# Second attention's scores: two full-height passes over stacked halves in place of three half-height passes

## The chip, the cores and the metric

The kernel runs on one core of one Trainium2 chip. The metric is the device time of one execution in microseconds (us), as the median of several runs. TensorE is called PE in the profile and its weight loads PEld; VectorE is DVE, ScalarE is ACT, GpSimd is POOL, SyncE is SP.

## What is computed

The reference runs a first block of two layers on 512 tokens of width 1024 (with 256 context tokens) and then a second block. The change lies in the attention of the second block, which has 8 dilated heads and 8 forgetting heads ("fox"), all of width 64:

```python
proj = h @ w_in[layer]
qa, ka, va, qf, kf, vf, f_pre = jnp.split(proj, splits, axis=-1)
o_dil = _dilated_attention(heads(qa, 8), heads(ka, 8), heads(va, 8), rel_bias)
log_f = jax.nn.log_sigmoid((f_pre + b_forget[layer]).astype(jnp.float32))
o_fox = _forgetting_attention(heads(qf, 8), heads(kf, 8), heads(vf, 8), log_f)
# inside, per query block of 128:
s = jnp.einsum('bqhd,bkhd->bhqk', qi, k) * SCALE      # the scores
s = s + ci[..., None] - c_k[:, :, None, :]            # fox; the dilated heads add a bias by distance
p = jax.nn.softmax(jnp.where(k_pos[None, :] <= q_pos[:, None], s, NEG_INF), axis=-1)
o = jnp.einsum('bhqk,bkhd->bqhd', p, v)
```

Behind it come an output projection, a router and 32 experts (two of which each token uses), and a final normalisation.

## The kernel before, in words

Matrix products that need more than one fp32r pass are split: a value x is held as hi (x rounded to fp32r) and lo (x - hi), and the product is hi·hi + lo·hi + hi·lo, three matmuls into one accumulator (`mm3`, L218 to L222: the lines L220, L221 and L222 are the three passes, whatever the product).

The second attention is `second_attention` (L1224). Its heads are taken two at a time, as groups g = 0 to 7 (0 to 3 dilated, 4 to 7 forgetting), a head being a step (g, e). All is written out straight, without loops on the chip. A compile-time scheduler lays out the order on each engine from the program's order and its own estimates of time; each engine then runs its queue in order, and waits on semaphores for its data. Only later, in the expert stage, is PE's order written out by hand.

- `late_consts` (L1186) makes `tri` (L1191, a triangle of ones for a cumulative sum) and `mask` from an index tile `jp`, which has the buffer tag `sqo`.
- `values` (L1196) projects the values of all heads. The forget gates' cumulative sum is `pcum` (L1260), which reads `tri`; its negative goes to `cs` (L1262) and by DMA to `cd`.
- `proj(g, a)` (L1270) projects the queries (a = 0) or the keys (a = 1) of one group: 24 matmuls of 128 x 512 into PSUM (`pqk`), then one ACT instruction to hi (L1281) and one DVE instruction to lo (L1282), each over 128 partitions: head e's 64 rows are partitions 64e to 64e + 63.
- `Fill` (L61) spreads the matmuls of the projections of later groups and, at the end, of half of the output projection (`dil_out`) between the steps of the heads, so that PE has other work while a head's softmax runs. `need(g)` forces what a head's scores require.
- `head_scores` (L1377) does one head: it loads F (the bias row, or the cumulative sums) by DMA on SP into one of two buffers, then the scores for four query blocks i with 128 (i + 1) keys each, three passes of 64 rows; forgetting heads add `mask` on the diagonal block by one more matmul with the identity, 128 rows high (L1399). DVE adds F and takes the maximum (L1406), ACT takes the exponential (L1408), POOL divides by the sum (L1411).
- `head_out` (L1414) turns the probabilities (`pPT`, L1425), splits them into PT2h (ACT) and PT2l (DVE), and multiplies by the values (`pO`, L1434). The scores of the next head are issued ahead of the transposes of this one.
- `nil` (L1330), also with the tag `sqo`, is filled with zeros by POOL and written by 16 DMAs on SP to `yd`, which the experts add to later. The loads of weights (`wraw`, L211) go through the same SP queue.

Of the kernel before, what the change touches and what calls it, by code (L numbers as in the profile page):

```python
# [10 lines left out]
F32 = mybir.dt.float32  # L11
F32R = mybir.dt.float32r
I32 = mybir.dt.int32
U32 = mybir.dt.uint32
AF = mybir.ActivationFunctionType
OP = mybir.AluOpType
# [95 lines left out]
class K:  # L112
# [1073 lines left out]
    def late_consts(self):  # L1186

        nc, pool = self.nc, self.bp
        jp = pool.tile([128, 512], F32, name="jp", tag="sqo", bufs=1)
        nc.gpsimd.iota(jp, pattern=[[1, 512]], base=0, channel_multiplier=-1, allow_small_or_imprecise_dtypes=True)  # L1190
        self.tri = pool.tile([128, 512], F32R, name="tri")  # L1191
        nc.vector.tensor_scalar(self.tri, jp, 0.0, None, op0=OP.is_ge)
        self.mask = pool.tile([128, 128], F32R, name="mask")
        nc.vector.tensor_scalar(self.mask, jp[:, :128], 0.0, -1e30, op0=OP.is_gt, op1=OP.mult)
# [29 lines left out]
    def second_attention(self, hT):  # L1224
        nc, I, sp = self.nc, self.I, self.sp
# [10 lines left out]
        for s, nm, n in ((0, "b_router_group_2", 4), (4, "b_router_expert_2", 32)):  # L1236
            a = I[nm][0]
# [11 lines left out]
        e = bp.tile([128, 4, 8], F32, name="fe")  # L1249
# [7 lines left out]
        p = self.pt("pcum")  # L1257
        for t in range(4):
            for k, x in enumerate((zh, zl)):
                nc.tensor.matmul(p[:8, t * 128:512], x[:, t, :], self.tri[:, :512 - t * 128],  # L1260
                                 start=(t == 0 and k == 0), stop=(t == 3 and k == 1))
        cs = bp.tile([8, 512], F32, name="cs")  # L1262
        nc.vector.tensor_scalar(cs, p[:8], -1.0, None, op0=OP.mult)
        cd = self.dr.tile([8, 512], F32, name="cd")
        nc.sync.dma_start(cd, cs)


        qk = [[None, None] for _ in range(8)]

        def proj(g, a):  # L1270
            c = (1536 if g >= 4 else 0) + a * 512 + (g % 4) * 128
            w = self.wunit(wi[:, :, c:c + 128], [128, 8, 128])
            yield 0
            p = self.pc("pqk")
            for k in range(8):
                self.mm3(p, [x[:, k, :] for x in w], [h[:, k, :] for h in hT], k == 0, k == 7)
                yield 0.64
            hi = bp.tile([128, 512], F32R, name="qk2h", tag=f"qh{a}", bufs=2)
            lo = bp.tile([128, 512], F32R, name="qk2l", tag=f"ql{a}", bufs=2)
            s = 1.0 if a else 0.125  # L1280
            nc.scalar.activation(hi, p, AF.Copy, scale=s)  # L1281
            nc.vector.scalar_tensor_tensor(lo, p, s, hi.bitcast(F32), op0=OP.mult, op1=OP.subtract)  # L1282
            qk[g][a] = (hi, lo)


        wo = I["w_out_2"][0].rearrange("(k p) n -> p k n", p=128)
# [2 lines left out]
        def dil_out(c0, t):  # L1289
# [5 lines left out]
            for k in range(4):  # L1295
# [3 lines left out]
            nc.vector.scalar_tensor_tensor(x, p, rsh[0][:, t:t + 1], x, op0=OP.mult, op1=OP.add)  # L1299

        late = Fill([proj(g, a) for g in range(8) for a in range(2)]
                    + [dil_out(c0, t) for c0 in (0, 512) for t in range(4)])

# [73 lines left out]
    def head_scores(self, g, e, qk, cd):  # L1377

        nc, sp, bp = self.nc, self.sp, self.bp
        fox = g >= 4  # L1380
        Q, Kt = qk
        b = e * 64
        hh = (g % 4) * 2 + e
        F = bp.tile([128, 512], F32, name="F", tag="F", bufs=2)
        if fox:
            s = cd[hh:hh + 1, :]
            nc.sync.dma_start(F, bass.AP(tensor=s.tensor, offset=s.offset, ap=[[0, 128], [1, 512]]))
        else:
            s = self.fd[hh]
            nc.sync.dma_start(F, bass.AP(tensor=s.tensor, offset=s.offset + 127, ap=[[639, 128], [1, 512]]))  # L1390
        P = bp.tile([128, 1280], F32, name="P2", tag="P2", bufs=2)
        p2, p3, p1 = (self.pb("pS2") for _ in range(3))
        pS = [p1[:, 0:128], p1[:, 128:384], p2[:, 0:384], p3]
        at = (0, 128, 384, 768)
        for i in (2, 3, 1, 0):
            L = 128 * (i + 1)
            self.mm3(pS[i], [x[b:b + 64, i * 128:(i + 1) * 128] for x in Q], [x[b:b + 64, :L] for x in Kt], True, not fox)
            if fox:
                nc.tensor.matmul(pS[i][:, i * 128:L], self.identr, self.mask, start=False, stop=True)  # L1399
        m = sp.tile([128, 4], F32, name="m2", bufs=3)  # L1400
        l = sp.tile([128, 4], F32, name="l2", bufs=3)
        Ps = [P[:, at[i]:at[i] + 128 * (i + 1)] for i in range(4)]
        for i in (2, 3, 1, 0):
            L = 128 * (i + 1)
            o = 0 if fox else 384 - 128 * i
            nc.vector.tensor_tensor_reduce(Ps[i], pS[i], F[:, o:o + L], 1.0, -3e38, OP.add, OP.max, m[:, i:i + 1])  # L1406
            nc.vector.tensor_scalar(m[:, i:i + 1], m[:, i:i + 1], -1.0, None, op0=OP.mult)  # L1407
            nc.scalar.activation(Ps[i], Ps[i], AF.Exp, bias=m[:, i:i + 1], accum_out=l[:, i:i + 1])  # L1408
        for i in (2, 3, 1, 0):
            nc.vector.reciprocal(l[:, i:i + 1], l[:, i:i + 1])  # L1410
            nc.gpsimd.tensor_scalar(Ps[i], Ps[i], l[:, i:i + 1], 1.0, op0=OP.mult, op1=OP.mult)  # L1411
        return Ps
# [751 lines left out]
```

## Time and profile before

| | us |
|---|---|
| median of 3 runs | 1468.28 |
| lowest, highest | 1463.38, 1468.56 |
| the profiled execution, its own time | 1465.97 |
| its span in the trace | 1464.0 |
| PE busy | 1335.9 (91%) |
| DVE busy | 951.9 (65%) |
| ACT busy | 595.9 (41%) |
| POOL busy | 310.0 (21%) |

The second attention from its first scores' projections to the last head takes the trace from about 884 to 1087 us, the dilated heads up to 979. "Busy" counts an instruction from its start to its modelled end; PE's matmuls overlap one another, so that two starts in a row tell more of a matmul's cost than its printed duration. A trailing bracket in a row gives the idle time of the engine before it and what ended it; "issue" means that nothing which the profile shows was waited for. [...]

### The profile page before, as it was taken

How to read it: one execution, taken by the hardware profiler on the slowest of the kernel's cores; microseconds unless marked ns; L12 is line 12 of the kernel's file. 1: busy time of each engine (PE TensorE's matmuls, PEld its weight loads, DVE VectorE, ACT ScalarE, POOL GpSimd, SP SyncE). 2: the span in 40 equal slices, each digit the busy share in tenths (PEclk: the TensorE clock that was granted, in tenths of full speed). 3: DMA queues.
4: the chain of work that ended last, by engine and by line, in shares of the span. 5: the costliest groups of instructions: out<-in, count | busy, mean ns of one | idle time of the engine just before them, and what ended most of it. 6: DMA issues, size and time to landing. Idle time of an engine off the chain costs nothing. (4 is left out here: it accounts for less than half of the span.)

```text
span 1464.0 us, 22692 instructions
## 1 busy us (share of the span) xinstructions
PE 1335.9 (91%) x8094; PEld 1055.6 (72%) x8094; DVE 951.9 (65%) x2253; ACT 595.9 (41%) x1166; POOL 310.0 (21%) x396
## 2 busy tenths in 40 slices
PE   4999989998979999799999899999998899999873
PEld 2888778876858788678877697887877777575441
DVE  4789986665743779998784545655567543454555
ACT  4543254534641564266572435654444111112112
POOL 2332042322220323133231201211110111111101
PEclk9999999999999999999999999999998899999987
DMA  8643453444142435433334454223436689999971
GB/s 297 191 134 101 116 153 116 128 121 150 45 143 63 123 95 160 126 94 105 89 109 144 135 177 127 73 80 115 165 113 233 199 295 365 378 368 391 383 278 58
DMA packets 166918, 246.48 MB, mean 168 GB/s; under 512 B 46774, under 2 KB 102918, under 8 KB 166804
## 3 DMA queue, kind: packets, MB, share of 16 engines
q1 hardware_dynamic: 161460, 235.07, 48.5%
q0 software_dynamic: 4768, 7.84, 1.9%
q10 hardware_dynamic: 576, 2.10, 0.4%
q8 instruction: 65, 1.06, 0.3%
q14 instruction: 49, 0.40, 0.1%
HBM read 221.74 MB, written 33.33 MB: 174 GB/s over the span
## 5 line engine op out<-in xcount | busy, mean ns | idle before, releaser
L184 DVE TENSOR_TENSOR wlo<-wraw,whi 128x1024 fp32r<-128x1024 f32 (+3 forms) x98 | 118.9, 1219 | 67.5 <-ACT whi L183 66.9
L183 ACT ACTIVATE whi<-wraw 128x1024 fp32r<-128x1024 f32 (+3 forms) x98 | 100.6, 1035 | 116.6 <-PE pout L222 42.6
L922 POOL TENSOR_SCALAR P<-P,ll 128x768 f32<-128x768 f32 (+1 forms) x80 | 76.2, 957 | 186.5 <-DVE ll L921 104.2
L220 PE MATMUL pcm<-hTh,whi 128*128 128x256 f32 (+1 forms) x288 | 102.9, 357 | 10.4 <-DVE oa L529 4.3
L569 DVE SCALAR_TENSOR_TENSOR za<-zp,vec,za 128x783 f32<-128x783 f32 (+1 forms) x120 | 109.2, 917 | 0.5
L222 PE MATMUL pcm<-hTh,wlo 128*128 128x256 f32 (+1 forms) x288 | 99.6, 346 | 0.2 <-DVE wlo L184 0.2
L221 PE MATMUL pcm<-hTl,whi 128*128 128x256 f32 (+1 forms) x288 | 98.7, 343 | 0.0
L184 DVE TENSOR_TENSOR PTl<-pPT,PTh 128x512 fp32r<-128x512 f32 x104 | 70.4, 683 | 23.7 <-ACT PTh L183 23.3
L183 ACT ACTIVATE PTh<-pPT 128x512 fp32r<-128x512 f32 x104 | 60.3, 595 | 54.9 <-PE pPT L935 46.9
L920 ACT ACTIVATE P<-pS,nm 128x768 f32<-128x768 f32 (+1 forms) x80 | 64.9, 814 | 34.5 <-DVE nm L918 30.1
L1411 POOL TENSOR_SCALAR P<-P,l 128x384 f32<-128x384 f32 (+1 forms) x64 | 33.3, 532 | 205.0 <-DVE m L1407 153.1
L1805 POOL DMA_INDIRECT xg<-h2d,tok x32 | 31.6, 988 | 208.3 <-PE pturn L1789 131.7
L917 DVE TENSOR_REDUCE nm<-pS 128x1 f32<-128x768 f32 (+1 forms) x80 | 66.4, 844 | 14.2 <-PE pS L222 13.4
L220 PEld LDWEIGHTS pcm<-hTh,whi 128*128 128x128 f32 x288 | 55.3, 192 | 18.2 <-DVE oa L529 4.9
L220 PE MATMUL pcm<-hT0h,whi 128*128 128x512 f32 x144 | 59.5, 413 | 7.9 <-DVE oa L529 5.8
L935 PE MATMUL pPT<-ident,P 128*128 128x128 f32 x416 | 63.4, 280 | 3.6 <-POOL P L922 2.9
L1822 PE MATMUL pgu<-exT,eraw 128*128 128x128 f32 x512 | 61.1, 280 | 0.0
L1822 PEld LDWEIGHTS pgu<-exT,eraw 128*128 128x128 f32 x512 | 59.5, 195 | 1.3 <-DVE exT L1800 0.6
L222 PEld LDWEIGHTS pcm<-hTh,wlo 128*128 128x128 f32 x288 | 55.2, 192 | 6.5 <-DVE wlo L184 0.6
L221 PEld LDWEIGHTS pcm<-hTl,whi 128*128 128x128 f32 x288 | 55.2, 192 | 4.8 <-issue 0.2
L221 PE MATMUL pcm<-hT0l,whi 128*128 128x512 f32 x144 | 58.1, 404 | 0.0
L222 PE MATMUL pcm<-hT0h,wlo 128*128 128x512 f32 x144 | 58.1, 403 | 0.0
(533 smaller groups left out, 3691.3 us busy)
## 6 DMA issues: line engine op xcount, KB each, us to landing
wraw<-in_w_in_dram SPq DMA_DIRECT2D x56, 512.0 KB
eraw<-in_w_expert_gate_dram SPq DMA_DIRECT2D x52, 512.0 KB
eraw<-in_w_expert_up_dram SPq DMA_DIRECT2D x52, 512.0 KB
wraw<-in_w_mod_dram SPq DMA_DIRECT2D x48, 512.0 KB
wl<-in_w_expert_down_dram SPq DMA_DIRECT2D x32, 512.0 KB
wh<-in_w_expert_down_dram SPq DMA_DIRECT2D x32, 512.0 KB
wraw<-in_w_out_dram SPq DMA_DIRECT2D x24, 512.0 KB
wraw<-in_w_expert_gate_dram SPq DMA_DIRECT2D x12, 512.0 KB
```

Of the source, the lines that this page charges most:

```text
L183: nc.scalar.activation(hi, src, AF.Copy)
L184: return (eng or nc.vector).tensor_tensor(lo, src, hi.bitcast(F32), op=OP.subtract)
L220: mm(out, lhs[0], rhs[0], start=start, stop=False)
L221: mm(out, lhs[0], rhs[1], start=False, stop=False)
L222: mm(out, lhs[1], rhs[0], start=False, stop=stop)
L569: nc.vector.scalar_tensor_tensor(a[:, :nz], z[:, k:k + nz], cfw[:, i, k:k + 1], a[:, :nz], op0=OP.mult, op1=OP.add)
L917: nc.vector.tensor_reduce(nm, S, axis=AX.X, op=OP.max, negate=True)
L920: nc.scalar.activation(P, S, AF.Exp, bias=nm, scale=SM1, accum_out=l)
L922: nc.gpsimd.tensor_scalar(P, P, l, 0.5, op0=OP.mult, op1=OP.mult)
L935: nc.tensor.transpose(p[:, jj, i * 128:(i + 1) * 128], Ps[i][:, (j + jj) * 128:(j + jj + 1) * 128], self.ident)
L1411: nc.gpsimd.tensor_scalar(Ps[i], Ps[i], l[:, i:i + 1], 1.0, op0=OP.mult, op1=OP.mult)
L1822: self.last = self.nc.tensor.matmul(p[:, s, c, :], gu[2 * s + k // 4][:, k % 4, c * 128:(c + 1) * 128], x[:, k, :], start=(k == 0), stop=( ...
```

## The change

A head's query tile becomes 128 rows high: its hi over its lo. The keys' hi is written twice, into the upper and the lower half of a tile; the keys' lo lies over zeros in one of three fixed tiles whose lower halves are zeroed once. Then queries times (hi, hi) gives hi·hi + lo·hi in one pass, and queries times (lo, 0) gives hi·lo in a second. The evacuation of a projection is done in halves of 64 partitions, one for each head, two of them moving rows from partitions 64 to 127 down to 0 to 63 or up. There are four query tiles and three key-hi tiles in rotation. `tri` and `cs` move into the two buffers of F, and a tile `zero` comes between `jp` and `nil` in the buffer `sqo`.

```diff
-        self.tri = pool.tile([128, 512], F32R, name="tri")
+        self.tri = pool.tile([128, 512], F32R, name="tri", tag="F", bufs=2)
...
-        cs = bp.tile([8, 512], F32, name="cs")
+        cs = bp.tile([128, 512], F32, name="cs", tag="F", bufs=2)[:8]
...
         qk = [[None, None] for _ in range(8)]
+        klo = [bp.tile([128, 512], F32R, name=f"klo{i}") for i in range(3)]
+        zero = bp.tile([128, 512], F32, name="zero", tag="sqo", bufs=1)
+        nc.gpsimd.memset(zero, 0.0)
+        for t in klo:
+            nc.vector.tensor_copy(t[64:128], zero[64:128])
...
-            hi = bp.tile([128, 512], F32R, name="qk2h", tag=f"qh{a}", bufs=2)
-            lo = bp.tile([128, 512], F32R, name="qk2l", tag=f"ql{a}", bufs=2)
+
+            x = [bp.tile([128, 512], F32R, name="qk2", tag=f"qk{a}", bufs=4 - a) for e in range(2)]
+            y = [klo[(2 * g + e) % 3] for e in range(2)] if a else [t[64:128] for t in x]
             s = 1.0 if a else 0.125
-            nc.scalar.activation(hi, p, AF.Copy, scale=s)
-            nc.vector.scalar_tensor_tensor(lo, p, s, hi.bitcast(F32), op0=OP.mult, op1=OP.subtract)
-            qk[g][a] = (hi, lo)
+            for e in range(2):
+                r = p[64 * e:64 * e + 64]
+                nc.scalar.activation(x[e][0:64], r, AF.Copy, scale=s)
+                if a:
+                    nc.scalar.activation(x[e][64:128], r, AF.Copy)
+                nc.vector.scalar_tensor_tensor(y[e][0:64], r, s, x[e][0:64].bitcast(F32), op0=OP.mult, op1=OP.subtract)
+            qk[g][a] = list(zip(x, y))
...
-        Q, Kt = qk
-        b = e * 64
+        Q, Kt = qk[0][e][0], qk[1][e]
...
-            self.mm3(pS[i], [x[b:b + 64, i * 128:(i + 1) * 128] for x in Q], [x[b:b + 64, :L] for x in Kt], True, not fox)
+            for k in range(2):
+                nc.tensor.matmul(pS[i], Q[:, i * 128:(i + 1) * 128], Kt[k][:, :L], start=(k == 0), stop=(k == 1 and not fox))
```

## Rows read from the trace of the kernel before

**Rows 1.** Windows by stage: us, each engine's busy time, PEclk, DMA share, GB/s

```profile
884.00:979.00 95.00, 93.78 (x487) 75.84 (x487) 56.18 (x183) 51.10 (x118) 16.56 (x32) 1.00 0.30 81
979.00:1087.00 108.00, 108.00 (x521) 85.73 (x519) 63.48 (x199) 52.49 (x119) 17.27 (x33) 0.94 0.33 113
...
1250.00:1350.00 100.00, 97.06 (x768) 63.94 (x760) 45.26 (x85) 17.25 (x33) 15.17 (x16) 1.00 1.02 381
```

**Rows 2.** Waits of PE and its loads, 884 to 1087: total us, times, longest

```profile
PEld pS L1399 <- issue: 4.9, 16, 0.4
PEld pS L220 <- issue: 4.7, 13, 0.4
...
PEld pPT L1425 <- POOL P L1411: 1.2, 1, 1.2
PEld pO L1434 <- ACT PT2h L183: 1.1, 2, 0.6
...
PEld pS L220 <- ACT qk2h L1281: 0.7, 2, 0.4
```

**Rows 3.** Timeline of PE, one dilated head's scores: start us, duration us, instruction

```profile
943.24 0.39 PE L221 MATMUL pqk<-hT1l,whi 128*128 128x512 f32 x1
943.47 0.40 PE L222 MATMUL pqk<-hT1h,wlo 128*128 128x512 f32 x1
943.80 0.44 PE L220 MATMUL pS<-qk2h 64*128 64x384 f32 x1
944.08 0.33 PE L221 MATMUL pS<-qk2l,qk2h 64*128 64x384 f32 x1
...
944.43 0.39 PE L220 MATMUL pS<-qk2h 64*128 64x512 f32 x1
...
945.13 0.27 PE L220 MATMUL pS<-qk2h 64*128 64x256 f32 x1
...
945.48 0.22 PE L220 MATMUL pS<-qk2h 64*128 64x128 f32 x1
945.53 0.28 PE L221 MATMUL pS<-qk2l,qk2h 64*128 64x128 f32 x1
945.65 0.27 PE L222 MATMUL pS<-qk2h,qk2l 64*128 64x128 f32 x1
945.85 0.33 PE L1425 MATMUL pPT<-ident,P 128*128 128x128 f32 x1
```

**Rows 4.** Timeline of PE and PEld, one forgetting head's scores

```profile
979.43 0.44 PE L220 MATMUL pS<-qk2h 64*128 64x384 f32 x1
...
983.01 0.40 PE L1425 MATMUL pPT<-ident,P 128*128 128x128 f32 x2
...
979.43 0.18 PEld L220 LDWEIGHTS pS<-qk2h 64*128 64x128 f32 x1 [0.36 <-issue]
...
980.15 0.19 PEld L1399 LDWEIGHTS pS<-mask,identr 128*128 128x128 f32 x1 [0.25 <-issue]
```

**Rows 5.** Windows of 1 us, PE alone: us, busy, PEclk, DMA share, GB/s

```profile
984.00:985.00 1.00, 1.00 (x5) 0.50 0.02 6
```

**Rows 6.** Groups by line and form, 884 to 1090: busy us, mean ns, idle before

```profile
L1281 ACT ACTIVATE qk2h<-pqk 128x512 fp32r<-128x512 f32 x15 | 8.9, 592 | 0.2
L1448 ACT ACTIVATE oT<-pO 64x512 f32<-64x512 f32 x15 | 8.9, 594 | 18.7 <-PE pO L1434 18.6
...
L1449 DVE TENSOR_TENSOR oT<-pO,oT 64x512 f32<-64x512 f32 x15 | 10.2, 679 | 8.3 <-ACT oT L1448 8.0
```

**Rows 7.** Timeline of SP, ACT and DVE around the stage's start

```profile
855.15 29.18 SPq L211 DMA_DIRECT2D wraw<-in_w_in_dram  x9
885.92 0.30 SPq L1265 DMA_DIRECT2D cd<-cs  x1
...
874.05 2.96 ACT L183 ACTIVATE whi<-wraw 128x1024 fp32r<-128x1024 f32 x3 [0.34 <-PE pv L222]
...
892.75 0.56 DVE L1406 CUSTOM_DVE_ANT_0 P<-pS,F 128x384 f32<-128x384 f32 x1 [1.30 <-PE pS L222]
```

## Prediction

> **What bounds the kernel now.** I read the windows by stage first. In the eight dilated heads (884 to 979 us) PE is busy 93.78 of 95 us, in the eight forgetting heads (979 to 1087) 108.00 of 108; VectorE is busy 56.18 and 63.48, ScalarE 51.10 and 52.49 [rows 1]. A busy PE is not a PE at its peak, so the waits come next: over the 203 us of both stages TensorE's waits for another engine at the transposes, at pO and at the scores add to 1.2 + 1.1 + 0.7 us, while "issue" ahead of the scores' and the mask's weight loads adds to 4.7 + 4.9 us [rows 2]. So the stage is as long as TensorE's instruction stream, and a microsecond taken out of that stream shortens it as long as the data for the next matmul are there. Last come the start times of single matmuls, because the printed durations (0.27 to 0.50 us) overlap: a matmul's cost is the time to the next start.
>
> **Removed: a third of the score passes.** A dilated head starts its scores at 943.80 and its transposes at 945.85: 2.05 us for 12 matmuls [rows 3]. The pitches: the last two 384-column passes (944.08 to 944.43) 0.175 each, 512 columns 0.70 / 3 = 0.23, 256 columns 0.35 / 3 = 0.12, 128 columns 0.12 (945.53 to 945.65). Ahead of the first stands a gap: the preceding projection matmul of 512 columns starts at 943.47, 0.33 before, where 0.23 is its pitch (943.24 to 943.47); 0.10 is lost on entering, and the 0.20 from 945.65 to 945.85 has 0.08 on leaving. No wait for data is named there; what changes is the height, 128 rows to 64 and back. In the forgetting heads the weight loads show it plainly: the load for the first score starts only with its own matmul, at 979.43, after 0.36 us of idle "issue", and the load for the mask, which is 128 high, after 0.25 [rows 4]; elsewhere the load runs under the matmul before. The mask comes after each of four row blocks, so the height changes eight times in such a head: 979.43 to 983.01, 3.58 us for 16 matmuls [rows 4].
>
> After the change all passes are 128 high. I take the full-height pass at the pitch of its column count, since the 512-column projection matmuls of 128 rows (0.23) and the 64-row passes of 512 columns (0.23) agree: streaming 128 rows instead of 64 adds nothing. Two passes per block: 2 x (0.175 + 0.23 + 0.12 + 0.12) = 1.29 us per head; a forgetting head has four masks of 128 columns more at 0.12, together 1.77.
> - Dilated: 2.05 + 0.10 - 1.29 = 0.86, x 8 = 6.9 us.
> - Forgetting: 3.58 + 0.10 (entry as in rows 3) - 1.77 = 1.91, x 8 = 15.3 us.
>
> Together 22.2 us. Bounds: if the mask keeps its gaps I lose 8 x 4 x 0.25 = 8 us of it; if the dilated heads whose passes lie apart lose more gaps than the one shown, 1 us comes on top.
>
> **The clock.** In the dilated stage the granted clock is 1.00, in the forgetting stage 0.94 [rows 1]. [...] Loss: 0.06 x 108 = 6.5 us. Ahead of each fall TensorE spent 3.6 us in the broken-up scores; the dilated heads, with 2.05 us and the same transposes behind, never fell. After the change a forgetting head's scores last 1.77 us without gaps, less than a dilated head's now. I take the whole 6.5 us back; the bounds are 0 and 6.5.
> [...]
>
> **Added: evacuations.** A projection is now evacuated in halves of 64 partitions: a query group by 2 ScalarE and 2 VectorE instructions, a key group by 4 and 2; before 1 and 1 each. A half costs no less than the whole: on ScalarE 128x512 takes 592 ns and 64x512 594; on VectorE 64x512 takes 679 [rows 6], and I take the whole at the same. Per group of two heads ScalarE gets 6 x 0.594 - 2 x 0.592 = 2.4 us more, VectorE 2 x 0.679 = 1.4; times 8: 19.0 and 10.9 us. The stage shrinks from 203 to about 175 us; ScalarE's 103.6 + 19 = 123 and VectorE's 119.7 + 11 = 131 fit, at 70 and 75%. What hides them is that projection matmuls fill TensorE between the steps of a head, and that a head's probabilities are made a whole head ahead of their transposes. What is late next: ScalarE runs in order, and four evacuations in a row (2.4 us) put the split of the transposed probabilities (PT2h), for which TensorE waits at pO, behind them; now that wait is 1.1 us [rows 2]. Bounds: 0, and the whole 19.0 us if TensorE stands for each added microsecond of ScalarE. I take 0.2 us for each of 16 evacuations, 3 us, near the low end, because the order is laid out around the instructions and that wait is near nothing now. The first scores of the first two groups need their group's evacuation at once (the wait for qk2h, 0.7 us in 2 [rows 2]); one more ScalarE instruction stands ahead of each: 2 x 0.6 = 1.2 us.
>
> **Moved: buffers at the start.** tri and cs now lie in F's two buffers. The first head's F can only be loaded when the cumulative-sum matmuls have read tri, the second's when cd is written from cs: after 885.92 instead of long before [rows 7]. Both loads queue on SP; behind them stands the next projection weight. VectorE needs the first F at 892.75 [rows 7], so there are 6.8 us for a 256 KB transfer, about 2 less for the second F, which is needed about 2 us later. TensorE waits 1.2 us for POOL behind that first head already [rows 2], so lateness there counts in full. Bounds 0 and 3; I take 1. The fill called zero waits on POOL for jp's readers, three VectorE copies wait for it, and the fill nil, next on POOL, waits for these copies; the 16 writes of yd on SP wait for nil, and behind them nine weight loads, from 855.15. Two fills and three copies at no more than 0.7 us each are 3.5 us; the first of these weights is split by ScalarE at 874.05, on TensorE's account [rows 7]. 19 us of cover: nothing. If the cover were gone, 3.5 us. The rotation of three key tiles adds a wait on the scores of a head two back, which are done by then: nothing.
>
> **Passing it on.** The stage behind moves its experts at 381 GB/s with a DMA share of 1.02 [rows 1] and could swallow a gain if its stream ran at its own time. But its weight loads start as buffers come free by TensorE's own progress; so it starts earlier by what attention saves. I take all of it.
>
> **Sum.** 22.2 + 6.5 - 3.0 - 1.2 - 1.0 = 23.5 us less. The profiled execution took 1465.97 us (span 1464.0), 2.3 under the median 1468.28. 1465.97 - 23.5 = 1442.5 us.
>
> **Rivals.**
> 1. The clock still falls, because the transposes stay. 23.5 - 6.5 = 17 us: 1449. For it: the falls lie at the transposes; against: the dilated heads have them too. [...]
> 2. ScalarE's longer blocks hold TensorE for half of the added 19 us, at pO: 9.5 instead of 3.0: 1449; with the clock still falling, 1455.5. Against: the near absence of such waits now.
> 3. Slower: the compiled order of TensorE puts the first score of a group ahead of its evacuation, as it does for the first two groups, and the whole chain stands in the open: a key group 4 x 0.594 + 0.679 = 3.1 us, a query group 2 x (0.594 + 0.679) = 2.5, times 8 = 45 us in place of the 3.0 + 1.2. Against it stand 22.2 + 6.5 - 1.0 = 27.7: 17 us slower, 1483. It decides from 27.7 / 16 = 1.7 us of standing per evacuation. Against: only 2 of 16 stood, for 0.7 us together.
> 4. It doesn't do what it says: the gain is eaten by the expert stage waiting for its transfers. No change, 1466. For it: the DMA share there; against: buffers, as above.
> 5. Full-height matmuls in a row can't load their weights under the one before. Then each of 8 x (8 + 12) pays a load of 0.19 [rows 4], 30 us: 1473. Against: the projection matmuls, all in the same 128 rows, keep 0.23 us [rows 3], which leaves no room for it: no chance. [...]
>
> **How the numbers follow.** Forecast (1434 to 1448) 0.58; rival 1 0.17; rival 2 0.13; rival 3 0.06; rival 4 0.06; rival 5 none. The range reaches from no cost at all with 1 us of gaps on top (29.7 us: 1436.3, less 2 for scatter) to rivals 1 and 2 together (1455.5) with 2.3 for the median's lead: 1434 to 1458; rivals 3 and 4 stay outside. Half a per cent is 7.3 us, about what a measurement of this kernel can tell from no change. Forecast and rivals 1 and 2 are faster by more: 0.88; rival 4 within: 0.06; rival 3 slower: 0.06.
>
> **What would show it.** A forgetting head's scores taking about 1.8 us from first score to first transpose and a dilated head's 1.3; no idle ahead of the mask's load; a granted clock near 1.00 in the forgetting heads; ScalarE's evacuations at 594 ns each; waits of TensorE for PT2h, for POOL and for the evacuations summing to no more than 8 us; the end of attention about 23 us earlier and the expert stage as long as before. The prediction is wrong if full-height pairs need more than their pitch here, if TensorE stands at pO or at the scores, or if the gain at the end of attention is gone at the end of the kernel.

## The result and the profile after

| | before | after |
|---|---|---|
| median of 4 runs, us | 1467.76 (1463.38 to 1468.56) | 1446.86 (1443.93 to 1447.81) |
| profiled execution, us (span) | 1465.97 (1464.0) | 1445.97 (1444.2) |
| second attention, us | 209.2 | 189.0 |
| ahead of it, us | 882.8 | 884.5 |
| behind it, us | 372.0 | 370.7 |

The ratio after / before is 0.9859, with a 95% interval of 0.9835 to 0.9882. The forecast was 1442.5 us in a range of 1434 to 1458: direction and range held, and the gain came out smaller than the forecast's, 20.0 us between the two profiled executions instead of 23.5.

"Second attention" is measured in every trace in the same way: from the start of the first cumulative-sum matmul to the start of the last pO matmul of a low half. The stretch ahead of it is the same work in all kernels of this study, and it ends at 881.5 to 886.8 us in their profiles. So one profile carries a scatter of some microseconds over 880; over the 200 us of the stage I lean on differences of 3 us and more, and on nothing below 2.

The windows of after (us; then the busy time of PE, PEld, DVE, ACT and POOL, each with its number of instructions; the granted TensorE clock, PEclk, where 1.00 is full speed; DMA share, GB/s): the dilated heads, the forgetting heads, and 100 us of the expert stage.

```profile
884.50:975.60 91.10, 88.86 (x461) 72.02 (x461) 64.63 (x194) 64.48 (x139) 17.46 (x32) 1.00 0.35 95
975.60:1073.50 97.90, 93.60 (x515) 77.56 (x514) 70.63 (x211) 60.96 (x135) 17.20 (x33) 1.00 0.41 137
1232.00:1332.00 100.00, 97.06 (x763) 63.96 (x760) 45.69 (x87) 17.28 (x34) 15.17 (x16) 1.00 1.01 379
```

Beside [rows 1], two things are to be seen. The forgetting heads now run at a granted clock of 1.00, where they had 0.94. And TensorE, which before was busy through all 108 us shown of them, now stands idle for 97.90 - 93.60 = 4.3 us of them, and for 2.2 in the dilated heads; VectorE and ScalarE have become busier. The expert stage has kept its rows.

The scores themselves, on TensorE's timeline of after (start, duration, instruction), a dilated head and then a forgetting one:

```profile
952.79 0.34 PE L1407 MATMUL pS<-qk,qk 128*128 128x384 f32 x1
952.96 0.34 PE L1407 MATMUL pS<-klo,qk 128*128 128x384 f32 x1
953.14 0.40 PE L1407 MATMUL pS<-qk,qk 128*128 128x512 f32 x1
...
954.01 1.06 PE L1435 MATMUL pPT<-ident,P 128*128 128x128 f32 x8
...
975.42 0.40 PE L222 MATMUL pqk<-hT1h,wlo 128*128 128x512 f32 x1
975.65 0.34 PE L1407 MATMUL pS<-qk,qk 128*128 128x384 f32 x1
975.83 0.34 PE L1407 MATMUL pS<-klo,qk 128*128 128x384 f32 x1
976.00 0.22 PE L1409 MATMUL pS<-mask,identr 128*128 128x128 f32 x1
976.06 0.44 PE L1407 MATMUL pS<-qk,qk 128*128 128x512 f32 x1
...
977.32 1.06 PE L1435 MATMUL pPT<-ident,P 128*128 128x128 f32 x8
```

952.79 to 954.01 is 1.22 us, where the head of [rows 3] took 2.05; 975.65 to 977.32 is 1.67 us, where the head of [rows 4] took 3.58. The first score follows the projection matmul after that one's pitch of 0.23, without the 0.10 lost on entering, and the mask's load no longer stands idle ahead of it (its group has 0.3 us of idle time over 32 loads).

What came in place of the "issue" rows of [rows 2] is the waits of TensorE's weight loads in the same stage of after (releaser: total us, times, longest):

```profile
PEld pO L1444 <- ACT PT2h L183: 5.3, 9, 1.2
PEld pO L1444 <- DVE PT2l L184: 4.9, 12, 0.9
PEld pO L1444 <- DVE m L1417: 3.4, 5, 1.3
PEld pS L1407 <- ACT qk L1291: 1.4, 3, 0.5
```

13.6 us at pO, against 1.1 + 0.7 before. A wait of a weight load runs in part under the matmul before it, so these add up to more than TensorE's own idle time at pO, which is 1.9 + 1.5 + 1.1 = 4.5 us; they tell where the stage waits, not by how much it is longer.

One such wait in full, on the timelines of after from 977 to 982 us (start, duration, instruction), first TensorE:

```profile
979.60 0.39 PE L1444 MATMUL pO<-PT2h,vst 128*128 128x512 f32 x1
...
980.29 0.40 PE L222 MATMUL pqk<-hT1h,wlo 128*128 128x512 f32 x1
981.52 0.51 PE L1444 MATMUL pO<-PT2l,vst 128*128 128x512 f32 x1 [0.84 <-DVE m L1417]
```

and VectorE in the same microseconds:

```profile
977.27 0.69 DVE L1292 SCALAR_TENSOR_TENSOR qk<-pqk,qk 64x512 fp32r<-64x512 f32 x1
977.98 0.56 DVE L1416 CUSTOM_DVE_ANT_0 P<-pS,F 128x384 f32<-128x384 f32 x1
...
978.47 0.69 DVE L1416 CUSTOM_DVE_ANT_0 P<-pS,F 128x512 f32<-128x512 f32 x1
...
979.19 0.69 DVE L1292 SCALAR_TENSOR_TENSOR qk<-pqk,qk 64x512 fp32r<-64x512 f32 x1
...
980.16 0.42 DVE L1416 CUSTOM_DVE_ANT_0 P<-pS,F 128x256 f32<-128x256 f32 x1
...
980.51 0.28 DVE L1416 CUSTOM_DVE_ANT_0 P<-pS,F 128x128 f32<-128x128 f32 x1
...
980.79 0.68 DVE L184 TENSOR_TENSOR PT2l<-pPT,PT2h 128x512 fp32r<-128x512 f32 x1
```

VectorE works without a pause through two evacuation halves (L1292) and the four additions of the next head's scores (L1416), and only then makes PT2l, the low half of the transposed probabilities; the pO matmul that reads it stands for 0.84 us. The row names "DVE m L1417" as the releaser, a 128x1 instruction that ended at about the same time; what pO reads is PT2l, which ended at 980.79 + 0.68 = 981.47, and pO starts at 981.52. In the trace of before, a head at 1037 us has pauses of 0.31 and 0.65 us between the same additions, because the longer scores deliver their blocks later, and PT2l follows 0.31 us after ScalarE's PT2h. That head has no evacuation in between; what the additions alone do on the head of 977 us is told with the third experiment.

### The profile page after: what moved, and what is told of

Its sections match the earlier page's. It is cut to its first block, busy times and chain, and to the rows that moved or that the text cites. A ratio compares the mean times of both kernels' runs of the same rounds, so it can differ in the third digit from the quotient of the medians.

```text
span 1444.2 us, 22627 instructions
## 1 busy us (share of the span) xinstructions
PE 1313.0 (91%) x8030; PEld 1039.8 (72%) x8030; DVE 963.3 (67%) x2272; ACT 614.8 (43%) x1198; POOL 311.3 (22%) x397
```

## The experiments

My theory after the comparison (A): the passes' height changes cost what the forecast said, and the missing 3.3 us went to the added evacuations. The rival (B): most of the new waits at pO come from the shorter scores alone, whose softmax now falls on top of the splits of the head before; a third possibility was that height had little to do with it and that a third of the passes simply went away.

### Height alone: the second pass over 64 rows

The second pass multiplies zeros in its lower 64 rows. Here it runs over the upper 64 rows alone: the same values, the same number of passes, but the height changes between every two.

```diff
 for k in range(2):
+    n = 64 if k else 128
-    nc.tensor.matmul(pS[i], Q[:, ...], Kt[k][:, :L], ...)
+    nc.tensor.matmul(pS[i], Q[:n, ...], Kt[k][:n, :L], ...)
```

> The changed kernel with its second pass (keys' low halves over zeros) run over 64 rows only: same passes, same columns, same result; only the height changes between matmuls. Theory (half the gain comes from the height changes that are gone): each block again goes 128, 64, 128, at about 0.27 us for there and back as in the rows of before (mask 0.26 late, 0.09 ahead of it), 64 blocks: 17 us slower than the changed kernel, 1463; loads idle by 'issue' ahead of the passes, and the granted clock of the forgetting heads falls below 1.00 again. Rival (the gain is the third pass alone, height is of no account): as the changed kernel, 1447 within 3.

Measured: 1457.47 us, ratio 0.9944 (0.992 to 0.9968); the stage is 9.7 us longer than in after, where 17 were expected. A forgetting head on TensorE's timeline of this kernel:

```profile
978.89 0.34 PE L1408 MATMUL pS<-qk,qk 128*128 128x384 f32 x1
979.15 0.44 PE L1408 MATMUL pS<-klo,qk 64*128 64x384 f32 x1
979.52 0.33 PE L1410 MATMUL pS<-mask,identr 128*128 128x128 f32 x1
979.68 0.44 PE L1408 MATMUL pS<-qk,qk 128*128 128x512 f32 x1
...
982.01 0.40 PE L1436 MATMUL pPT<-ident,P 128*128 128x128 f32 x2
```

and the waits of its weight loads over the stage (total us, times, longest):

```profile
PEld pS L1408 <- issue: 9.8, 38, 0.4
PEld pS L1410 <- issue: 3.4, 16, 0.2
...
PEld pO L1445 <- DVE PT2l L184: 1.1, 5, 0.3
PEld pO L1445 <- ACT PT2h L183: 0.4, 1, 0.4
```

The 384-column pair takes 0.26 + 0.37 us to the next starts, in after 0.18 + 0.17. The head lasts 3.12 us (after 1.67), a dilated one whose passes lie together 2.63 (after 1.22). In three dilated heads the passes lie apart and lose less; summed over all 16 heads, from the start of each score or mask matmul to the next start, it is 43.2 us instead of 23.9: 19.3 us more of score time for the same passes. Height does cost, and "issue" is the row where it shows. But the stage grew by 9.7, half of that, and the waits at pO fell from 13.6 to 1.5 us: slower scores give VectorE and ScalarE the time back. The clock stayed at 1.00, so the part of the expectation that saw it fall was wrong.

### Number alone: three passes, all 128 high

```diff
-for k in range(2):
-    nc.tensor.matmul(..., start=(k == 0), stop=(k == 1 and not fox))
+for n, k in enumerate((0, 1, 1)):
+    nc.tensor.matmul(..., start=(n == 0), stop=(n == 2 and not fox))
```

The term of the keys' low halves is counted twice in this kernel.

> The changed kernel with its second pass run twice, so that queries' high times keys' low counts double: three full-height passes. Theory: a pass costs its columns, 0.175 + 0.23 + 0.12 + 0.12 = 0.65 us per head, 16 heads: 10 us slower than the changed kernel, 1457, and still 10 faster than before; clock 1.00 in the forgetting heads. Rival (TensorE isn't the bound there any more, since it waits at pO for VectorE and ScalarE): less than 4 us slower, 1451 or under. Rival (the third pass is the whole gain): as before, 1467.

Measured: 1458.71 us, ratio 0.9937 (0.9913 to 0.9961); the stage is 9.4 us longer than in after, at a clock of 1.00. A third full-height pass over 1280 columns per head is 0.645 x 16 = 10.3 us by the pitches, so nearly all of it is seen, with 11.7 us of waits at pO left. Number and height both count.

### The passes without the evacuations, and the evacuations without the passes

Two kernels start from before. The first replaces only the passes: two of 128 rows on the unchanged tiles. It mixes two heads' rows and leaves out the queries' low halves; its evacuations are those of before.

```diff
-self.mm3(pS[i], [x[b:b + 64, ...] for x in Q], [x[b:b + 64, :L] for x in Kt], True, not fox)
+for k in range(2):
+    nc.tensor.matmul(pS[i], Q[0][:, ...], Kt[k][:, :L], start=(k == 0), ...)
```

> The kernel before with its scores as two full-height passes over the unstacked tiles (queries' high times keys' high, then times keys' low, over both heads' 128 rows at once): this mixes the two heads and leaves out queries' low; the evacuations stay as before, one per engine. Theory A (the added evacuations cause the waits at pO that ate about 6 us): 1441, 6 faster than the changed kernel, waits at pO under 4 us together. Theory B (the waits come from the shorter scores, which bring a head's softmax on top of the split of the transposed probabilities): 1447 within 2, waits at pO about 14 us as in the changed kernel. The routing to experts may differ with the values; only the attention stage is then compared.

The second keeps the three passes of before and evacuates in halves, with a copy of the keys' high halves that nobody reads, and with tri and cs in F's buffers.

```diff
+dup = bp.tile([128, 512], F32R, name="dup", tag="dup", bufs=1) if a else None
+for e in range(2):
+    h = slice(64 * e, 64 * e + 64)
-    nc.scalar.activation(hi, p, AF.Copy, scale=s)
+    nc.scalar.activation(hi[h], p[h], AF.Copy, scale=s)
+    if a:
+        nc.scalar.activation(dup[h], p[h], AF.Copy)
     ...
```

> The kernel before, three half-height passes, with projections evacuated in halves as in the changed kernel (and a copy of each key half into a tile that nothing reads), tri and cs in F's buffers. Theory A (added evacuations stand on TensorE's account): 1472 to 1477, 4 to 9 slower than before. Theory B (they are covered, the waits come from the shorter scores): 1467 within 2.

Measured: 1446.37 us, ratio 0.9863 (0.9831 to 0.9895), and 1467.37 us, ratio 1.0015 (1.0001 to 1.003). In the first the mixed heads change what the experts are given to do (375.6 us behind attention instead of 370.7), so its stage is compared and not its total. The stages of the four kernels:

| us in second attention | evacuations as before | in halves |
|---|---|---|
| three passes of 64 rows | 209.2 (before) | 210.2 |
| two passes of 128 rows | 184.1 | 189.0 (after) |

With the long scores the evacuations in halves cost 1.0 us, which one pair of profiles does not tell from nothing (the whole kernel's ratio puts it at 0.1 to 4.4 us); with the short ones 4.9. The granted clock was 0.97 over both stages with long scores and 1.00 over both with short ones, so neither difference comes from it. The waits at pO (releaser: total us, times, longest) of the kernel with the passes alone:

```profile
PEld pO L1435 <- DVE PT2l L184: 3.8, 11, 0.7
PEld pO L1435 <- ACT PT2h L183: 3.1, 5, 1.0
PEld pO L1435 <- DVE m L1408: 2.9, 6, 0.9
```

and of the one with the evacuations alone:

```profile
PEld pO L1439 <- DVE PT2l L184: 1.7, 5, 0.5
PEld pO L1439 <- ACT PT2h L183: 0.6, 1, 0.6
```

9.8 of after's 13.6 us stand there without a single added evacuation. The head shown above for after has its counterpart in the kernel with the passes alone: its four additions run back to back from 977.68 to 979.44, PT2l starts only at 979.50 although PT2h had ended at 978.49, and pO stands 0.32 us, in after 0.84. Another of its heads shows the same on ScalarE: four exponentials from 1035.49 to 1037.79, PT2h at 1037.81, and pO stands 0.61 us. Rival B is right on where most of the waits come from, and theory A on what the evacuations add. Neither alone gives the whole loss.

### Filling the wait

Where TensorE stands at pO, projection matmuls could run if the program's order put them there. One kernel shifts projection time from the end of a head (FB, in us of TensorE time) to the three places ahead of its uses of the transposed probabilities (FA at each), 6.0 us in all as before; one lets GpSimd write the second copy of the keys' high halves; one does both; and one shifts the fill in the kernel before.

```diff
-FA, FB = 1.2, 2.4
+FA, FB = 1.8, 0.6
```

```diff
-                    nc.scalar.activation(x[e][64:128], r, AF.Copy)
+                    nc.gpsimd.tensor_copy(x[e][64:128], x[e][0:64])
```

> The changed kernel with the same projection work between heads, more of it ahead of each use of the transposed probabilities (FA 1.8 instead of 1.2 at each of three places) and less at the head's end (FB 0.6 instead of 2.4). Theory (what is left of the loss is TensorE reaching pO before ScalarE and VectorE have split the probabilities, about 8 us): waits at pO fall from 13.4 to under 5 us and the time by 4 to 8, to 1439 to 1443. Rival (the loss sits elsewhere, in the evacuations ahead of the scores): 1447 within 2.

> The changed kernel with the second copy of the keys' high half made by GpSimd from the first one, not by ScalarE from PSUM: 16 instructions of 0.59 us less on ScalarE. Theory (the added evacuations cost 4.9 us in the attention stage, through ScalarE's order): half of that back, 1444.5. Rival (it is VectorE's added half, 11 us of work, that costs): 1447 within 1.5.

> Both of the last two edits in the changed kernel. If they act on different waits: 1437 to 1441; if on the same wait at pO, no better than the better of the two alone.

> The kernel before with the shifted fill (FA 1.8, FB 0.6). Theory (waits at pO came only with the shorter scores): nothing to gain, 1466 within 3. Rival (the old split of the fill was poor in itself): 1460 or less.

| | us | ratio to before | second attention, us |
|---|---|---|---|
| after, shifted fill | 1441.78 | 0.985 (0.9818 to 0.9882) | 185.1 |
| after, copy on GpSimd | 1445.03 | 0.9883 (0.9857 to 0.9909) | 187.3 |
| after, both | 1443.03 | 0.9865 (0.9843 to 0.9887) | 185.3 |
| before, shifted fill | 1470.97 | 1.0043 (1.0013 to 1.0072) | 213.6 |

The shifted fill takes 3.9 us off the stage. Its waits of weight loads at pO are 8.9 us, more than expected:

```profile
PEld pO L1444 <- ACT PT2h L183: 4.5, 7, 1.0
PEld pO L1444 <- DVE PT2l L184: 3.7, 10, 0.9
PEld pO L1444 <- DVE m L1417: 0.7, 2, 0.5
```

It removes most of the waits that the rows put to "m", as the one in which VectorE had a whole head's additions ahead of PT2l (3.4 to 0.7), and leaves the others. At the level of the whole kernel its interval overlaps that of after, so it is not shown to be faster.

The same shift makes the kernel before slower, which neither theory had expected, but not by its waits: those at pO are 0.6 us from 886 to 1068 us, where before has 1.5 from 883 to 1065. It is the clock. The windows of the whole stage, before and then before with the shifted fill:

```profile
882.84:1092.00 209.16, 207.94 (x1038) 166.44 (x1037) 124.49 (x389) 106.41 (x241) 33.83 (x65) 0.97 0.33 103
885.70:1099.30 213.60, 212.73 (x1038) 171.60 (x1038) 124.83 (x389) 106.24 (x241) 34.05 (x65) 0.94 0.31 98
```

By these the clock takes, as an estimate, 0.03 x 209 = 6 us from the one and 0.06 x 214 = 13 us from the other, and the stages differ by 4.4. So the old fill is not shown to suit the old scores better in itself; shifting it made the clock fall more (0.94 instead of 0.97), in the other executions too: six of this kernel read a mean clock of 0.954 to 0.964, the nine of before beside them 0.964 to 0.965.

With the copy on GpSimd, measured between its two expectations, ScalarE gets 9 us lighter (123 to 114 us busy), but the stage gains only 1.7, less than I rely on, and in its waits of weight loads the scores wait for the new writer:

```profile
PEld pS L1407 <- POOL qk L1291: 2.0, 2, 1.0
```

Both together are no better than the fill alone.

### The clock and the height

In the forgetting heads of before the granted clock falls to 0.50 in four places, the one of [rows 5] and these (windows of 1 us, TensorE alone):

```profile
998.00:999.00 1.00, 1.00 (x6) 0.50 0.42 164
1025.00:1026.00 1.00, 1.00 (x6) 0.50 0.00 0
1066.00:1067.00 1.00, 1.00 (x6) 0.50 0.80 274
```

The heads' scores ahead of them run from 979.43 to 983.01, 993.33 to 996.90, 1021.08 to 1024.78 and 1062.06 to 1065.74 us, and the first microsecond below 1.00 begins at 983, 997, 1024 and 1065. Two kernels look at what TensorE did before its clock fell; the theories are that a long stretch broken by height changes is enough (L), or that half height is enough (H). The first runs after's two full passes and then the second once more over 64 rows (the low halves of the keys counted twice): long score stretches with height changes. The second is before with the mask's matmul over the same 64 rows as the scores (it leaves out the mask for half the queries): half height throughout, without changes inside a head's scores.

```diff
-for k in range(2):
+for n, (k, h) in enumerate(((0, 128), (1, 128), (1, 64))):
-    nc.tensor.matmul(pS[i], Q[:, ...], Kt[k][:, :L], ...)
+    nc.tensor.matmul(pS[i], Q[:h, ...], Kt[k][:h, :L], ...)
```

```diff
-nc.tensor.matmul(pS[i][:, i * 128:L], self.identr, self.mask, start=False, stop=True)
+nc.tensor.matmul(pS[i][:, i * 128:L], self.identr[b:b + 64, :], self.mask[b:b + 64, :], start=False, stop=True)
```

> Three passes, two full-height and a third over 64 rows (keys' low halves again, so that this product counts double): a forgetting head's scores should last about 3.12 + 0.65 = 3.8 us, as long as in the kernel before (3.58) and with eight height changes as there. Theory L (the clock fell because of a long stretch broken up by height changes): the clock falls in the forgetting heads, 0.93 to 0.97 in that stage. Theory H (it fell because nearly all of the stretch ran at half height): 1.00. Attention about 10 us longer than in the kernel with the half-height second pass, 208 us.

> The kernel before with the mask's matmul over 64 rows, the same 64 as the head's scores (the mask of half of the queries is left out): no height change inside a head, three half-height passes. A forgetting head's scores: 3 x 0.65 + 4 x 0.12 = 2.4 us instead of 3.58, so that attention is 9 us shorter, 200 us, if the clock is as before. Theory L: with the breaks gone and the stretch short, the granted clock is 1.00 in the forgetting heads. Theory H: it still falls there. The routing to experts may differ with the values; only attention is compared.

Measured: 1470.15 us, ratio 1.0025 (1.0001 to 1.0049), stage 211.5; and 1456.93 us, ratio 0.9938 (0.9915 to 0.9961), stage 197.2. Windows of the forgetting heads, first of the kernel with the pass added, then of the one with the half mask:

```profile
987.00:1090.00 103.00, 102.48 (x513) 79.80 (x512) 66.65 (x204) 58.43 (x130) 17.25 (x33) 1.00 0.34 118
```

```profile
978.00:1079.00 101.00, 100.04 (x548) 82.21 (x547) 66.41 (x205) 54.72 (x123) 17.30 (x33) 1.00 0.39 132
```

TensorE's timeline of a head in the kernel with the half mask:

```profile
978.67 0.44 PE L220 MATMUL pS<-qk2h 64*128 64x384 f32 x1
978.96 0.33 PE L221 MATMUL pS<-qk2l,qk2h 64*128 64x384 f32 x1
...
979.31 0.22 PE L1399 MATMUL pS<-mask,identr 64*128 64x128 f32 x1
979.37 0.45 PE L220 MATMUL pS<-qk2h 64*128 64x512 f32 x1
...
981.18 0.33 PE L1425 MATMUL pPT<-ident,P 128*128 128x128 f32 x1
```

The clock stayed at 1.00 in both. A long stretch broken by height changes (989.00 to 992.77, 3.77 us, in the first) did not make it fall, and half height alone did not either: L and H both fell. In the second kernel, though, a head's stretch was also shorter (2.51 us instead of 3.58). The clock fell in the three kernels that have three half-height passes and a mask of full height between them: before (0.94 in the forgetting heads), the evacuations alone (0.97 in either half of the stage), and before with the shifted fill, whose forgetting heads read:

```profile
981.20:1099.30 118.10, 118.10 (x546) 94.90 (x546) 67.52 (x206) 53.62 (x122) 17.34 (x33) 0.88 0.31 109
```

But the mask is not needed for a fall. In the kernel with the evacuations alone the first one lies in the dilated heads, which have no mask; twelve half-height passes in a row (893.13 to 895.67) and three more from 896.10 stand ahead of it:

```profile
896.50:903.00 6.50, 6.50 (x22) 4.80 (x21) 3.12 (x24) 4.47 (x15) 4.16 (x8) 0.50 0.31 81
```

Nor is a long half-height stretch enough: the first two dilated heads of before run 21 such passes in a row (892.10 to 895.55, 3.45 us) at 1.00. And with the same scores the shifted fill alone made the clock fall more (0.88 in the forgetting heads instead of 0.94). So what stands between the score stretches counts too, and what brings a fall is not settled.

The half mask also prices the mask. The head takes 978.67 to 981.18, 2.51 us instead of 3.58: of the 15.3 us forecast for the forgetting heads, 1.07 x 8 = 8.6 hung on the mask being the one matmul of another height. With the clock that is 15.1, and the stage became 12.0 us shorter; here too the waits at pO grew with the shorter scores, from 1.8 to 6.1 us. The height of that one matmul, clock included, is worth more than half of what the whole change brought in this stage.

## Why the prediction was nearly right, point by point

- **Passes removed, 22.2 us: shown.** The heads take 1.67 and 1.22 us, forecast 1.77 and 1.29. Full height keeps the pitch of the column count (952.79 to 952.96 for 384 columns), so rival 5 fell. If the 0.10 and 0.07 us hold for all 16 heads, it was 23.5 us. They do, nearly: summed from start to next start over all score and mask matmuls, it is 45.7 us before and 23.9 after, and with 0.10 for each of 16 entries 23.4 us less.
- **Height as the cause of the gaps: shown**, by the half-height second pass (19.3 us more score time with the passes unchanged in number) and by the half mask. The price is 0.28 us for the 384-column pair with one change in and one out (0.26 + 0.37 against 0.18 + 0.17).
- **Clock, 6.5 us: right in size, but by luck.** 1.00 in the stage; rival 1 fell: all eight transposes per head stayed, and the clock no longer fell. The forecast's reason, that the length of the broken scores brings the falls, fell: 3.77 us of them left the clock at 1.00, and a dilated head without a mask had a fall. Its remark that the dilated heads have 2.05 us overlooked that the first two run together for 3.45 us in before. What brings the falls is not settled.
- **The costs: 5.2 us forecast, 8.5 measured** (22.2 + 6.5 - 20.2; 9.8 with the shorter heads). This is the step that was mis-sized, and the four kernels of the table say which term. Added evacuations: forecast 3.0 + 1.2 + 1.0 = 5.2, measured 4.9 as after less the passes alone. Inside it pO's waits grew from 9.8 to 13.6 us (forecast 3.0); the scores' waits for their evacuation went from 0.7 to 1.4 us, where 1.2 more were forecast; from the first cumulative-sum matmul to the first transposes it took 15.24 us instead of 14.94 (14.12 with the passes alone), where F was to cost 1.0; but the first addition that reads F, at 894.02, had waited for the scores and not for F. So the sum of the added evacuations came out right, and not each of its terms.
- **The term that was missing, 3.6 us:** with the evacuations of before, two full passes shorten the stage by 25.1 us, not by 28.7. The prediction set the condition itself ("as long as the data for the next matmul are there") but asked it only of the evacuations. Shorter scores bring a head's additions on VectorE and exponentials on ScalarE earlier, onto the splits PT2h and PT2l of the head before, as the two heads of the kernel with the passes alone show; their own time does not shrink with the scores.
- **"ScalarE runs in order ... PT2h": half of it.** ScalarE's PT2h ends 5.3 of the 13.6 us; the rest is put to VectorE, which got 10.9 us more work in the forecast and no wait. Rival 2's time, 1449, is nearer to 1446.9 than the forecast's 1442.5, but not by its mechanism: all added evacuations together cost 4.9 us and not 9.5, and what was missing came from the shorter scores.
- **Waits of no more than 8 us:** exceeded, 13.6 at pO alone; the sign named for it was the right one to look at. The idle time of TensorE itself is 6.5 us in the stage, 4.5 of it at pO.
- **Evacuations at 594 ns:** measured below. **yd, zero, klo, nil at nothing:** held; no wait for the fills or for their copies stands among TensorE's. The one wait that names klo (0.8 us, a `pdo` matmul at 1032.93) is for the evacuation of a key's low half.
- **Passing on:** held. 372.0 us behind attention before, 370.7 after, with the rows of the expert stage unchanged: rival 4 fell. Rival 3 fell: three waits of scores for evacuations, 1.4 us in all.

The evacuation groups of after (busy us, mean ns of one, idle before), ScalarE's of high halves and of the second copies, and VectorE's of low halves:

```profile
L1289 ACT ACTIVATE qk<-pqk 64x512 fp32r<-64x512 f32 x32 | 18.9, 591 | 9.0 <-DVE qk L1292 7.7 <-DVE klo L1292 0.9
L1291 ACT ACTIVATE qk<-pqk 64x512 fp32r<-64x512 f32 x16 | 9.5, 592 | 0.2
L1292 DVE SCALAR_TENSOR_TENSOR qk<-pqk,qk 64x512 fp32r<-64x512 f32 x16 | 11.0, 689 | 1.1 <-ACT qk L1289 0.7
```

The halves cost what the whole cost in [rows 6] (592 ns), also where they move from partitions 64 to 127 down to 0 to 63: the shortest and the longest of the 32 differ by 24 ns (573 to 597).

Left open: why the clock fell, and how the 3.6 us divide between VectorE's additions and ScalarE's exponentials, which no run took apart. In the kernel with the passes alone TensorE's own idle time at pO, 2.5 us, is put to PT2h for 1.3 and to VectorE for 1.2.

## What to carry to other kernels

Keep neighbouring matmuls at one height: a full-height mask among half-height passes cost 1.07 / 4 = 0.27 us by its height, more than a 512-column pass (0.23), and it shows as "issue" idle ahead of weight loads (4.9 us ahead of the mask's in [rows 2]), not as a wait for anyone. When a stage is as long as TensorE's stream, a cut in the stream is worth its length only as far as the engines that feed the next matmul have slack at that place (here 25.1 us of 28.7 without any added evacuation), so ask of the cut itself, not only of what is added, whose work now arrives on top of whose. Afterwards look again at an order that was tuned for the old lengths: with the short scores a shifted fill took 3.9 us off the stage. And look at the granted clock before calling an order slower: the same shift in the old kernel cost clock (0.94 over the stage instead of 0.97) and not waits.

## What the runs showed of the hardware that was not expected

- A pass of 64 rows between passes of 128 costs more than one of 128: the 384-column second pass takes 0.37 us to the next start at 64 rows and 0.17 at 128, and the pass ahead of it 0.26 instead of 0.18.
- In the second attention the granted clock fell below 1.00 (to 0.50 in [rows 5]) only in kernels with three half-height passes a head and a full-height mask in the forgetting ones (0.94, 0.97 and 0.88 there), once in a dilated head without a mask; height changes for 3.77 us a head, scores and mask at half height, and 3.45 us of half-height passes in a row left it at 1.00.
- Evacuations nearly free beside long scores (1.0 us for 17.8 more of ScalarE's and 11.8 of VectorE's busy time) cost 4.9 beside short ones, with both engines below 75% busy in the stage's windows.
